# Decode steps kept on GpSimd, and the second groups' B and C projected before the last x tiles

## The chip, the cores and the metric

One core of a Trainium2 chip runs the whole program; the metric is device microseconds of one execution, and less is better. The core has a matrix engine (TensorE, PE in the rows; its weight loads are PEld), VectorE (DVE), ScalarE (ACT), GpSimd (POOL) and SyncE (SP), whose queue issues most DMAs. Each engine works through its own list of instructions in order and waits on semaphores for the others.

## The reference

One step of a hybrid layer (d_model 1024) for a prompt of 1024 positions and 8 decode requests of one position each, all with the same weights. Cut to what the change touches:

```python
proj = rmsnorm(x) @ w_in                       # columns: z (1536) | x,B,C (2048) | dt (24) | v (512)
xbc  = silu(causal_dwconv(xbc, width 4))       # x: 24 heads x 64; B, C: 4 groups x 64
y    = ssd_scan(x, dt, a, B, C, h0) + d_skip * x          # chunks of 128 positions
y    = rmsnorm(y * silu(z), per group of 384) * w
x    = x + concat(y, pooling(v)) @ w_out ;  then the convolutional FFN
```

For a decode request the scan is one step: `h = exp(dt*a)*h0 + dt*x*B`, `y = sum over the 64 states of h*C`, plus `d_skip*x`; `h` is an output. There are 12 tiles of x with 128 channels each, so 12 such steps on tiles of 128 x 8 requests x 64 states.

## The kernel before

Channels lie on the 128 partitions and the 1032 positions (1024 of the prompt, 8 of decode) in the free dimension. Every product is made of three float32r matmuls (high x high, high x low, low x high), L159 to L161. A projected tile is 128 output channels: three groups of 24 matmuls of 344 columns, 72 in all, and each group gets a PSUM bank (`g`) that ScalarE empties. The input tiles are numbered as in `w_in`: 0 to 11 are x, 12 and 13 are B, 14 and 15 are C, 16 to 27 are z (the gate tiles). Tile 12 and 14 serve the first half of the heads (x tiles 0 to 5), 13 and 15 the second half (x tiles 6 to 11).

`conv_tile` projects one of the tiles 0 to 15: weights are loaded (L130, SP), split into high and low parts (L140 on ScalarE, L141 on VectorE), projected, evacuated to `u` (L468 to L471, ScalarE), convolved into `xs` (L481 on ScalarE, then three L483 on VectorE), and passed through SiLU (L188, ScalarE). `gate_tile` projects a z tile, evacuates it (L656), applies SiLU and multiplies it into `xs` on VectorE (L661 for the prompt, L663 for the 8 decode columns). After every third gate tile a group norm adds up squares on GpSimd (L676) and sums them over partitions with matmuls (L683).

The scan over 8 chunks of 128 positions is done for the first half of the heads (q = 0) and then for the second (q = 1). For a chunk, `decay` loads a table of cumulated decays (`mix`, by DMA), clamps it on VectorE (L505), takes exponentials on ScalarE and multiplies the part for the incoming state (`ce`) by C on GpSimd (L520). `turn` transposes x, B and C on TensorE (L532, L538, L541). `apply` makes the chunk's products (L564, L587, L597), scales the state `h` on GpSimd (L573), adds to it on VectorE (L577), and adds the products to `xs` on VectorE (L605). A chunk's `ce` must be there before its L597, and `h` of the chunk before it too.

`sample_tile` is the decode step of one x tile: five operations on GpSimd (L636 to L639, L641, 128 x 512 elements except L636), a load and a store of the state `st`, and then on VectorE the sum over the 64 states (L642) and the skip term (L643). `st`, the scratch tile `stt` and the broadcast B and C (`bc`) have one buffer each. The tile `bcs`, through which B and C of a half reach DRAM (`sample_bc`, L617 on VectorE), uses the same buffer as `stt`.

`ssd_phase` sets the program's order. Scan steps and decode steps stand in a queue; before each of a tile's three groups of matmuls, `between` adds a credit and calls as many steps as whole credits allow. In the code's order: x tiles 1 to 5; the first half's chunks between the groups of x tiles 6 to 11; decode steps 0 to 5 between those of tiles 13 and 15; the second half's chunks, with decode steps 6 to 11 in steps 1 to 6 of them, between those of gate tiles 16 to 21. Gate tiles 22 to 27 and the pooling tiles follow outside the phase. A scheduler then fixes each engine's list from that order and its own estimate of times, so an engine's list is not the code's order; the lists are compared below.

```python
        for n in range(6, 12):
            self.keep(n, self.conv_tile(n, n, between))
        flush()
```

Of the kernel before, what the change touches and what calls it, by code (L numbers as in the profile page):

```python
# [13 lines left out]
ALU = mybir.AluOpType  # L14
AX = mybir.AxisListType
# [10 lines left out]
NST = 64  # L26
# [49 lines left out]
class Kernel:  # L76
# [543 lines left out]
    def sample_tile(self, q, i):  # L620

        nc, d = self.nc, self.d
        g = (i // 3) % 2
        if i % 3 == 0:
            self.bc = self.ph.tile([P, 2, NB, NST], F32, tag="bc", name=self.nm("bc"), bufs=1)
            for j in range(2):
                src = self.bcd[q : q + 1, :, j * P + g * NST : j * P + (g + 1) * NST]
                nc.sync.dma_start(self.bc[:, j], src.rearrange("o b n -> (o b) n").partition_broadcast(P))
        bb, cc = self.bc[:, 0], self.bc[:, 1]
        xt = self.xs_samp(self.xs[i])  # L630
        st = self.ph.tile([P, NB, NST], F32, tag="st", name=self.nm("st"), bufs=1)
        nc.sync.dma_start(st, d["st_ssm"][i])
        dx = self.ph.tile([P, 2, NB], F32, tag="dx", name=self.nm("dx"), bufs=2)
        tmp = self.ph.tile([P, NB, NST], F32, tag="stt", name=self.nm("stt"), bufs=1)
        bcast = lambda a: a.unsqueeze(2).broadcast_to([P, NB, NST])
        nc.gpsimd.tensor_tensor(out=dx[:, 0], in0=self.dtS[:, i, :], in1=xt, op=ALU.mult)  # L636
        nc.gpsimd.tensor_tensor(out=tmp, in0=bb, in1=bcast(dx[:, 0]), op=ALU.mult)
        nc.gpsimd.tensor_tensor(out=st, in0=st, in1=bcast(self.dA[:, i, :]), op=ALU.mult)
        nc.gpsimd.tensor_tensor(out=st, in0=st, in1=tmp, op=ALU.add)  # L639
        nc.sync.dma_start(d["ssm_s"][i], st)  # L640
        nc.gpsimd.tensor_tensor(out=tmp, in0=st, in1=cc, op=ALU.mult)  # L641
        nc.vector.tensor_reduce(out=dx[:, 1], in_=tmp, axis=AX.X, op=ALU.add)  # L642
        nc.vector.scalar_tensor_tensor(  # L643
            out=xt, in0=xt, scalar=self.c("dsk", i), in1=dx[:, 1], op0=ALU.mult, op1=ALU.add
        )

    def gate_tile(self, n, i, between):
        nc = self.nc
# [47 lines left out]
    def project(self):  # L696

        nc, d, tc = self.nc, self.d, self.tc
        self.bcd = self.dram.tile([2, NB, 2 * P], F32, name="bcd")
        self.xs, self.bt, self.ctl = [None] * XT, {}, {}  # L700

        with ExitStack() as outer:
            with self.banks(g=3, pT=2, pY=2, pM=1) as self.ps:
                self.startup([(n, n) for n in (12, 14, 0)])
                self.pu = outer.enter_context(tc.tile_pool(name="u", bufs=1))
                with tc.tile_pool(name="ssd", bufs=1) as self.ph:
                    self.ssd_phase()
            with self.banks(g=4, pT=2, pY=1, pM=1) as self.ps, tc.tile_pool(name="mix", bufs=1) as self.ph:
                for i in range(6, 12):
                    self.gate_tile(16 + i, i, None)  # L710
                self.pool_groups()

    def ssd_phase(self):
        nc, d = self.nc, self.d
        self.hst = {}
        queue = []

        credit = [0.0, 0.0]

        def between():  # L720
            credit[0] += credit[1]
            while credit[0] >= 1.0 and queue:
                credit[0] -= 1.0
                queue.pop(0)()
            if not queue:
                credit[0] = 0.0

        def flush():
            while queue:
                queue.pop(0)()  # L730

        def ssd_tasks(q):
            dec, trn = {}, {}

            def start():
                dec[0] = self.decay(q, 0)

            def step(c):
                if c >= 0:
                    self.apply(q, c, *dec.pop(c), *trn.pop(c))  # L740
                if c + 1 < NCH:
                    trn[c + 1] = self.turn(q, c + 1, dec[c + 1][0])
                if c + 2 < NCH:
                    dec[c + 2] = self.decay(q, c + 2)
                if c == -1:
                    self.sample_bc(q)
                if q == 1 and 1 <= c < 7:
                    sample(5 + c)

            queue.append(start)  # L750
            for c in range(-1, NCH):
                queue.append(lambda c=c: step(c))

        def sample(i):
            with self.behind(self.pl):
                self.sample_tile(i // 6, i)

        self.lo_eng = nc.gpsimd
        for n in range(1, 6):
            self.keep(n, self.conv_tile(n, n, None))  # L760
        ssd_tasks(0)
        credit[:] = 0.35, 0.6
        for n in range(6, 12):
            self.keep(n, self.conv_tile(n, n, between))
        flush()
        self.lo_eng = nc.vector
        for i in range(6):
            queue.append(lambda i=i: sample(i))
        credit[1] = 1.0
        for n in (13, 15):  # L770
            self.keep(n, self.conv_tile(n, n, between))
        flush()
        nc.sync.dma_start(d["conv_o"], self.conv_st)
        ssd_tasks(1)
        credit[:] = 0.35, 0.6
        for i in range(6):
            self.gate_tile(16 + i, i, between)
        flush()
        self.run_due()
# [789 lines left out]
```

## Time and profile before

| | us |
|---|---|
| median of 3 runs | 1425.16 (1421.04 to 1427.28) |
| the profiled execution | 1422.84 |
| its span, first to last instruction | 1421.1 |
| TensorE busy | 1364.8 (96%) |
| VectorE busy | 968.7 (68%) |
| ScalarE busy | 701.1 (49%) |
| GpSimd busy | 504.5 (36%) |

Times in the rows count from the start of the span. A matmul's record lasts longer than its share of the array, since matmuls are pipelined, so the pace is read from starts. The granted clock is a share of TensorE's full clock: 1.00 is 2.4 GHz and 0.50 is 1.2 GHz. The stretch that the change touches runs from about 232 us, after the last chunk of the first half, to about 407 us, after the last chunk of the second half.

### The profile page before, as it was taken

The numbers are of one execution on the slowest core, as the hardware profiler recorded it, in microseconds if no ns is written. First come the engines' busy times: TensorE is split into PE (matmuls) and PEld (weight loads), VectorE is DVE, ScalarE is ACT, GpSimd is POOL, SyncE is SP. The second block draws the span as 40 slices with busy tenths as digits, with TensorE's granted clock in tenths as the row PEclk, the third lists the DMA queues.
The fourth block names the chain that finished last, engine by engine and source line by source line (L and its number), as shares of the span: only waits on it lengthen the run. The fifth ranks groups of instructions, "written<-read, shape, count | busy, mean of one in ns | idle before, by whom it ended". The sixth has DMA issues, their size and how long they took to land.

```text
span 1421.1 us, 26585 instructions
## 1 busy us (share of the span) xinstructions
PE 1364.8 (96%) x10312; PEld 1313.3 (92%) x10312; DVE 968.7 (68%) x1474; ACT 701.1 (49%) x1408; POOL 504.5 (36%) x577
## 2 busy tenths in 40 slices
PE   8999999797999999999989999999999999999997
PEld 6899878786789999999978999999999999999997
DVE  6474899578853385563589777777777786567743
ACT  6247774276454543221455555545554555445451
POOL 5243466547631103776232222222122224214122
PEclk9999999999899999999999999999999999999999
DMA  6031334334311127776576878787777869657513
GB/s 246 9 100 56 102 113 164 120 116 127 127 40 40 34 76 265 237 236 220 152 196 146 219 194 203 192 195 180 182 196 201 202 202 324 223 185 236 179 54 120
DMA packets 126811, 227.56 MB, mean 160 GB/s; under 512 B 27980, under 2 KB 45212, under 8 KB 126684
## 3 DMA queue, kind: packets, MB, share of 16 engines
q1 hardware_dynamic: 86316, 139.39, 31.4%
q0 software_dynamic: 24336, 61.30, 17.6%
q10 hardware_dynamic: 16032, 25.16, 5.3%
q8 instruction: 81, 1.33, 0.4%
q14 instruction: 46, 0.38, 0.1%
HBM read 169.11 MB, written 45.15 MB: 151 GB/s over the span
## 4 chain that ended last, share of the span: by engine, by line
PE 79%; DVE 10%; DMA 4%; issue 3%; POOL 2%; ACT 1%; SPq 0%; DVEq 0%; ACTq 0%; POOLq 0%
PE g L1074 30%; PE g L1256 15%; PE g L160 10%; PE g L161 10%; PE g L159 10%; DMA mix<-acd 1%; DVE wop L141 1%; DVE xs L483 1%; DVE mix L550 1%; PE pY L587 1%; DMA st<-st_ssm 1%; DVE x L296 1%; DVE xs L605 1%; DVE mix L505 1%; POOL st L639 1%
## 5 line engine op out<-in xcount | busy, mean ns | idle before, releaser
L1074 PE MATMUL g<-op,wop 128*128 128x258 f32 x3696 | 445.3, 283 | 4.7 <-ACT op L999 1.7
L1074 PEld LDWEIGHTS g<-op,wop 128*128 128x128 f32 x3696 | 444.1, 189 | 5.7 <-DVE op L1004 2.0
L140 ACT ACTIVATE wop<-raw 128x512 fp32r<-128x512 f32 (+1 forms) x208 | 125.9, 608 | 225.3 <-PE g L161 131.9
L159 PE MATMUL g<-hh,wop 128*128 128x344 f32 x696 | 226.5, 325 | 4.4 <-ACT u L468 3.0
L1256 PE MATMUL g<-op,wop 128*128 128x258 f32 x1848 | 225.2, 283 | 2.4 <-ACT op L210 1.7
L1256 PEld LDWEIGHTS g<-op,wop 128*128 128x128 f32 x1848 | 222.7, 189 | 3.5 <-ACT op L210 1.9
L161 PE MATMUL g<-hh,wop 128*128 128x344 f32 x696 | 225.8, 324 | 0.0
L160 PE MATMUL g<-hl,wop 128*128 128x344 f32 x696 | 225.2, 324 | 0.0
L141 DVE TENSOR_TENSOR wop<-raw,wop 128x512 fp32r<-128x512 f32 (+1 forms) x186 | 141.3, 765 | 110.5 <-ACT wop L140 108.3
L140 ACT ACTIVATE wop<-s 128x512 fp32r<-128x512 f32 (+1 forms) x136 | 83.6, 620 | 139.6 <-PE g L1256 52.0
L159 PEld LDWEIGHTS g<-hh,wop 128*128 128x128 f32 x696 | 132.1, 190 | 7.6 <-ACT u L468 3.6
L161 PEld LDWEIGHTS g<-hh,wop 128*128 128x128 f32 x696 | 132.1, 190 | 1.9 <-issue 1.7
L160 PEld LDWEIGHTS g<-hl,wop 128*128 128x128 f32 x696 | 132.4, 190 | 0.7 <-issue 0.7
L1054 POOL DMA_DIRECT2D s<-s x44 | 38.3, 870 | 258.2 <-DVE wop L141 111.0
L1156 DVE SCALAR_TENSOR_TENSOR acc<-u,cst,acc 128x1048 f32<-128x1048 f32 x88 | 115.2, 1309 | 12.2 <-ACT acc L1154 10.6
L141 DVE TENSOR_TENSOR wop<-s,wop 128x512 fp32r<-128x512 f32 (+1 forms) x136 | 92.0, 682 | 36.2 <-ACT wop L140 34.2
L1134 DVE TENSOR_TENSOR u<-u,g 128x258 f32<-128x258 f32 (+2 forms) x176 | 58.0, 354 | 72.9 <-PE g L1074 66.1
L1131 ACT ACTIVATE u<-g 128x258 f32<-128x258 f32 (+2 forms) x220 | 69.6, 340 | 70.7 <-PE g L1074 70.6
L160 PE MATMUL g<-yl,wop 128*128 128x344 f32 x288 | 91.9, 320 | 1.6 <-DVE yl L211 1.6
L161 PE MATMUL g<-yh,wop 128*128 128x344 f32 x288 | 91.8, 320 | 0.0
L159 PE MATMUL g<-yh,wop 128*128 128x344 f32 x288 | 91.1, 320 | 0.0
L1226 POOL DMA_DIRECT2D g<-td x77 | 41.8, 548 | 122.3 <-DVE op L211 70.6
(269 smaller groups left out, 2278.2 us busy)
## 6 DMA issues: line engine op xcount, KB each, us to landing
s<-wup SPq DMA_DIRECT2D x88, 256.0 KB, 3.5
g<-td POOLq DMA_DIRECT2D x77, 258.0 KB, 4.7
raw<-wup SPq DMA_DIRECT2D x66, 256.0 KB, 4.1
raw<-win SPq DMA_DIRECT2D x58, 256.0 KB, 2.6
mix<-acd SPq DMA_DIRECT2D x16, 768.0 KB, 6.5
td<-acc ACTq DMA_DIRECT2D x22, 516.0 KB, 6.1
s<-wup POOLq DMA_DIRECT2D x44, 256.0 KB, 5.6
s<-s POOLq DMA_DIRECT2D x44, 256.0 KB, 3.9
```

The lines of the kernel that those rows point to most:

```text
L140: self.nc.scalar.activation(hi, raw[:, :w], AF.Copy)
L141: lo_eng.tensor_tensor(out=lo, in0=raw[:, :w], in1=hi.bitcast(F32), op=ALU.subtract)
L159: nc.tensor.matmul(ps[:, :n], wh, xh[:, sl], start=(first and k == 0), stop=False)
L160: nc.tensor.matmul(ps[:, :n], wh, xl[:, sl], start=False, stop=False)
L161: nc.tensor.matmul(ps[:, :n], wl, xh[:, sl], start=False, stop=(final and k == last))
L1054: nc.gpsimd.dma_start(t, raw[acc] if acc in raw else w[acc][j], accum_op=ALU.add)
L1074: nc.tensor.matmul(out, a, b, start=(p in OPENS and j == 1), stop=(j == 12), skip_group_check=True)
L1131: a = nc.scalar.activation(out, ps[:, s], AF.Copy, scale=-1.0 if p in ("p5", "p4") else 1.0)
L1134: nc.vector.tensor_tensor(out=out, in0=out, in1=ps[:, s], op=op)
L1156: nc.vector.scalar_tensor_tensor(out=acc, in0=u[:, k : k + FW], scalar=self.c("fw", 3 * n + k), in1=acc, op0=ALU.mult, op1=ALU.add)
L1226: self.loaded = self.nc.gpsimd.dma_start(st[:, j], self.td[i + j][ROW[p]]).ins
L1256: self.pe = nc.tensor.matmul(out, a, b, start=(s == 0 and i == 0 and j == 0), stop=(s == len(PIECES) - 1 and i == nk - 1 and j == 2),).ins
```

## The change

Three things. The decode step's last two operations leave VectorE: GpSimd sums the 64 states by six halving additions (32, 16, 8, 4, 2 and 1 wide) and makes the skip term with two more, eight instructions in place of two. Tiles 13 and 15 are projected among the first half's chunks, in place of x tiles 10 and 11, which come behind them with the decode steps, at a credit of 0.7 in place of 1.0 and with no flush. One gate tile (16) stands between x tile 11 and the second half's chunks, which lie between gate tiles 17 to 22; 23 to 27 remain outside.

```diff
-        nc.vector.tensor_reduce(out=dx[:, 1], in_=tmp, axis=AX.X, op=ALU.add)
-        nc.vector.scalar_tensor_tensor(
-            out=xt, in0=xt, scalar=self.c("dsk", i), in1=dx[:, 1], op0=ALU.mult, op1=ALU.add
-        )
+        w = NST
+        while w > 1:
+            w //= 2
+            out = dx[:, 1].unsqueeze(2) if w == 1 else tmp[:, :, :w]
+            nc.gpsimd.tensor_tensor(out=out, in0=tmp[:, :, :w], in1=tmp[:, :, w : 2 * w], op=ALU.add)
+        nc.gpsimd.tensor_scalar(out=xt, in0=xt, scalar1=self.c("dsk", i), scalar2=None, op0=ALU.mult)
+        nc.gpsimd.tensor_tensor(out=xt, in0=xt, in1=dx[:, 1], op=ALU.add)
...
-                for i in range(6, 12):
+                for i in range(7, 12):
                     self.gate_tile(16 + i, i, None)
...
-        for n in range(6, 12):
+        for n in (13, 15, 6, 7, 8, 9):
             self.keep(n, self.conv_tile(n, n, between))
         flush()
...
-        credit[1] = 1.0
-        for n in (13, 15):
+        credit[1] = 0.7
+        for n in (10, 11):
             self.keep(n, self.conv_tile(n, n, between))
-        flush()
         nc.sync.dma_start(d["conv_o"], self.conv_st)
+
         ssd_tasks(1)
+        self.gate_tile(16, 0, between)
         credit[:] = 0.35, 0.6
-        for i in range(6):
+        for i in range(1, 7):
             self.gate_tile(16 + i, i, between)
```

The new lines shift the code behind them by three or four: L661 and L663 become L664 and L666, L676 becomes L679, L683 becomes L686, L656 becomes L659.

On VectorE, this is a piece of the difference at the end of the first half's chunks, where the weights' low parts (`wop`), the convolution of the next tile (`xs_2421`) and the sums of decode steps 1 and 2 (`dx`, from `stt`) stand:

```order
-L505 SCALAR_TENSOR_TENSOR mix_2807<-acl,mix_2807 128x1536
-L642 TENSOR_REDUCE dx_2484<-stt_2485 128x8
-L643 SCALAR_TENSOR_TENSOR xs_784<-xs_784,cst,dx_2484 128x8
+L505 SCALAR_TENSOR_TENSOR mix_2935<-acl,mix_2935 128x1536
 L141 TENSOR_TENSOR wop_2567<-raw_2565,wop_2567 128x512
 L141 TENSOR_TENSOR wop_2572<-raw_2570,wop_2572 128x512
-L483 SCALAR_TENSOR_TENSOR xs_2421<-u_2298,cst,xs_2421 128x1056
-L642 TENSOR_REDUCE dx_2522<-stt_2523 128x8
-L483 SCALAR_TENSOR_TENSOR xs_2421<-u_2298,cst,xs_2421 128x1056
-L643 SCALAR_TENSOR_TENSOR xs_883<-xs_883,cst,dx_2522 128x8
-L483 SCALAR_TENSOR_TENSOR xs_2421<-u_2298,cst,xs_2421 128x1056
+L483 SCALAR_TENSOR_TENSOR xs_2421<-u_2298,cst,xs_2421 128x1056 x3
```

The sums are gone, and the three convolution steps follow each other.

On ScalarE, before, from the last convolved tile (`xs_2697`, tile 15, the second half's C) to the exponentials of the second half's chunks 0 and 1 (`mix_2742`, `mix_2807`); `z` is gate tile 16, `bT` is B transposed for chunk 0:

```order
L481 ACTIVATE xs_2697<-u_2575,cst 128x1056
L656 ACTIVATE z_2740<-g_2715 128x344
L188 ACTIVATE xs_2697<-xs_2697 128x1056
L181 ACT_TABLE_LOAD
L188 ACTIVATE mix_2742<-mix_2742,acl 128x128 x12
L656 ACTIVATE z_2740<-g_2758 128x344
L533 ACTIVATE bT_2786<-pM_2787 128x128
```

And after the change, where `xs_2697` is x tile 11, `z_2740` again gate tile 16, `z_2868` gate tile 17, and `mix_2870` and `mix_2935` belong to chunks 0 and 1:

```order
L481 ACTIVATE xs_2697<-u_2575,cst 128x1056
L659 ACTIVATE z_2740<-g_2715 128x344
L188 ACTIVATE xs_2697<-xs_2697 128x1056
L659 ACTIVATE z_2740<-g_2760 128x344
L140 ACTIVATE wop_2989<-raw_2987 128x512
L659 ACTIVATE z_2740<-g_2804 128x344
L140 ACTIVATE wop_2994<-raw_2992 128x512
L188 ACTIVATE z_2740<-z_2740 128x1032
L181 ACT_TABLE_LOAD
L188 ACTIVATE mix_2870<-mix_2870,acl 128x128 x12
L188 ACTIVATE mix_2935<-mix_2935,acl 128x128 x2
L659 ACTIVATE z_2868<-g_2843 128x344
```

A whole gate tile now lies between the last SiLU that the chunks need and the transposed B of chunk 0 (`bT`, some rows further on).

On TensorE the same place counts in matmuls: from the end of the first half's last chunk, 240 matmuls stood before the first transpose of the second half (L532) and 26 more before the first that needs C (L538); now 312 stand before L532 and L538 follows at once. From the second half's chunk 0 (L564) to its chunk 7, 307 matmuls of projections stood between the chunks, and 288 now.

On GpSimd, before, from the scaled state (`h`) of the second half's chunk 3 over decode step 8 (`dx_3409`, `st_3407`, `stt_3410`) to the state of chunk 4:

```order
L573 TENSOR_TENSOR h_3330<-h_3164,cd 128x384
L636 TENSOR_TENSOR dx_3409<-dtS,xs_1776 128x8
L638 TENSOR_TENSOR st_3407<-st_3407,dA 128x512
L520 TENSOR_TENSOR ce_3099<-ce_3099,xs_2697 128x768
L637 TENSOR_TENSOR stt_3410<-bc_3117,dx_3409 128x512
L676 TENSOR_TENSOR sq_3318<-sq_3318,sq_3319 128x1056
L639 TENSOR_TENSOR st_3407<-st_3407,stt_3410 128x512
L641 TENSOR_TENSOR stt_3410<-st_3407,bc_3117 128x512
L573 TENSOR_TENSOR h_3493<-h_3330,cd 128x384
```

And after the change, from decode step 7's product with C to the state of chunk 3:

```order
L641 TENSOR_TENSOR stt_3384<-st_3381,bc_3252 128x512
L646 TENSOR_TENSOR stt_3384<-stt_3384 128x8x32
L646 TENSOR_TENSOR stt_3384<-stt_3384 128x8x16
L646 TENSOR_TENSOR stt_3384<-stt_3384 128x8x8
L646 TENSOR_TENSOR stt_3384<-stt_3384 128x8x4
L646 TENSOR_TENSOR stt_3384<-stt_3384 128x8x2
L646 TENSOR_TENSOR dx_3383<-stt_3384 128x8
L648 TENSOR_TENSOR xs_2039<-xs_2039,dx_3383 128x8
L520 TENSOR_TENSOR ce_3234<-ce_3234,xs_1513 128x768
L679 TENSOR_TENSOR sq_3163<-sq_3163,sq_3164 128x1056
L573 TENSOR_TENSOR h_3486<-h_3305,cd 128x384
```

Seven more small operations (with L647, the skip term's product, further up) now stand ahead of the next chunk's `ce`, the group norm's sum and the next `h`.

## Rows read from the trace of the kernel before

**Rows 1.** The page's first line.

```profile
span 1421.1 us, 26585 instructions
```

**Rows 2.** Stretches: us; busy us of PE, PEld, DVE, ACT, POOL; granted clock; DMA.

```profile
232.50:274.00 41.50, 38.49 (x248) 37.84 (x241) 28.00 (x34) 13.35 (x24) 26.95 (x27) 1.00 0.46 141
274.00:283.90 9.90, 4.47 (x29) 4.16 (x27) 4.72 (x6) 1.10 (x2) 3.75 (x4) 0.96 0.44 140
283.10:289.90 6.80, 5.98 (x24) 5.76 (x25) 4.13 (x7) 6.77 (x19) 0.00 (x0) 0.50 0.01 2
293.40:407.00 113.60, 102.20 (x780) 84.02 (x780) 97.08 (x144) 63.99 (x134) 74.82 (x47) 0.89 0.38 119
320.70:327.50 6.80, 5.46 (x42) 3.66 (x43) 5.46 (x8) 5.32 (x15) 5.17 (x4) 0.50 0.13 47
378.80:395.80 17.00, 17.00 (x92) 11.74 (x90) 15.40 (x25) 9.62 (x19) 12.16 (x7) 0.50 0.37 127
407.00:720.00 313.00, 311.17 (x2035) 307.32 (x2033) 161.85 (x234) 117.29 (x191) 116.30 (x119) 1.00 0.47 151
```

**Rows 3.** Waits from 232 to 290 us: total us, times, longest us.

```profile
ACT xs L188 <- DVE xs L483: 38.3, 4, 10.1
DVE dx L642 <- POOL stt L641: 13.6, 4, 4.4
...
PE pT L538 <- ACT xs L188: 5.4, 1, 5.4
...
PE g L159 <- ACT u L468: 3.0, 2, 2.3
```

**Rows 4.** The chain that ended last, 278 to 287 us: start, us, what.

```profile
278.21 1.24 POOL stt L641
279.47 0.69 DVE dx L642
...
281.53 1.23 DVE xs L483
282.78 1.09 ACT xs L188
283.92 0.80 PE pT L538 x4
...
286.19 0.29 PE g L161
```

**Rows 5.** TensorE in order of time, first and last of 34 matmuls.

```profile
239.78 0.32 PE L159 MATMUL g<-hh,wop 128*128 128x344 f32 x1
...
244.98 0.32 PE L159 MATMUL g<-hh,wop 128*128 128x344 f32 x1
```

**Rows 6.** GpSimd by line, 290 to 410 us: busy us, mean ns, idle before.

```profile
L641 POOL TENSOR_TENSOR stt<-st,bc 128x512 f32<-128x512 f32 x6 | 11.8, 1970 | 0.4
...
L636 POOL TENSOR_TENSOR dx<-dtS,xs 128x8 f32<-128x8 f32 x6 | 2.5, 408 | 0.0
```

**Rows 7.** GpSimd, 225 to 285 us: one long product; ns min/median/max of the small one.

```profile
278.18 1.26 POOL L641 TENSOR_TENSOR stt<-st,bc 128x512 f32<-128x512 f32 x1
...
L636 POOL TENSOR_TENSOR dx<-dtS,xs x4: 209/398/1209, 239.3 to 264.1; 128x8 f32<-128x8 f32 x4
```

**Rows 8.** VectorE by line, 290 to 410 us.

```profile
L642 DVE TENSOR_REDUCE dx<-stt 128x8 f32<-128x512 f32 x6 | 4.1, 678 | 3.7 <-POOL stt L641 3.7
...
L643 DVE SCALAR_TENSOR_TENSOR xs<-xs,cst,dx 128x8 f32<-128x8 f32 x6 | 1.7, 278 | 0.0
```

**Rows 9.** VectorE in order of time: one operation twice, GpSimd idle, then busy.

```profile
347.42 1.76 DVE L505 SCALAR_TENSOR_TENSOR mix<-acl,mix 128x1536 f32<-128x1536 f32 x1 [3.02 <-DMA mix<-acd]
...
390.91 2.83 DVE L505 SCALAR_TENSOR_TENSOR mix<-acl,mix 128x1536 f32<-128x1536 f32 x1
```

**Rows 10.** Waits of TensorE from 225 to 425 us.

```profile
PE pY L597 <- POOL ce L520: 3.4, 1, 3.4
...
PE pM L532 <- DVE h L577: 2.8, 1, 2.8
```

## The prediction

> **What bounds the kernel now.** The first line of the page gives the span, 1421.1 us [rows 1]; the execution takes 1422.84 us, so 1.7 us lie around it. Next I cut the span into stretches [rows 2]. From 407 to 720 us TensorE is busy for 311.17 of 313.00 us at a granted clock of 1.00: there the matmuls themselves are the time, and whatever arrives there earlier is won in full. The pace is 0.158 us a matmul: 34 of them start between 239.78 and 244.98, 33 steps in 5.20 us [rows 5]. Before 407 us TensorE waits, in two places.
>
> The first is the end of the decode steps. From 274.00 to 283.90 us TensorE is busy for only 4.47 of 9.90 us [rows 2]. The waits of this stretch tell who is waited for [rows 3]: TensorE stands 5.4 us before the transpose that needs C (L538), waiting for ScalarE's SiLU of that tile, and 3.0 us for a bank that ScalarE has yet to empty (L468). ScalarE in turn stands 38.3 us, in four waits, for VectorE's convolution, and VectorE 13.6 us for GpSimd, at the sum over the states. The chain that ended last shows it link by link [rows 4]: GpSimd's product with C at 278.21, VectorE's sum at 279.47, the convolution to 282.76, SiLU at 282.78, TensorE's transpose at 283.92. VectorE takes its list in order, so the convolution of a tile waits for a decode step that has nothing to do with it. Then TensorE's clock is granted at 0.50, its lower level of 1.2 GHz, from 283.1 to 289.9 us [rows 2], right after the engine stood idle; a matmul takes 0.29 us there [rows 4].
>
> The second is the stretch of the second half's chunks, 293.4 to 407 us. No single engine fills its 113.6 us: VectorE is busy for 97.08 and GpSimd for 74.82 [rows 2], and they hand work to each other in every chunk. TensorE's list waits for `ce` from GpSimd (3.4 us) and for `h` from VectorE (2.8 us), among others [rows 10], and the clock is at 0.50 for 6.8 and 17.0 us [rows 2].
>
> **The change part by part.** *The sums and skip terms leave VectorE, and the order of tiles changes.* Both act on the first place, so I cost them together. With the sums gone, VectorE's convolution no longer waits for GpSimd; and tiles 13 and 15, whose B and C the transposes need, are done long before, while after the last x tile there are 48 + 72 matmuls, 120 x 0.158 = 19.0 us, before the first transpose. Undisturbed, SiLU follows a tile's last matmul after an evacuation, a step on ScalarE and three L483 of 1.23 us [rows 4]; I estimate 8 us, so it is covered. What goes is the 5.4 and the 3.0 us [rows 3], and half of the 5.98 busy us at 0.50 [rows 2], 3.0 us: **11.4 us**. The lower bound is nothing, if a new wait takes their place; the cover is 46 more matmuls (312 against 266), 7.3 us, and if the decode steps ended so late that this were used up, GpSimd's list would hold the chunks' `ce` back. Before, GpSimd's last product of the six steps ended at 279.4 [rows 7], and its waits for VectorE go while the additions come, so I expect it to end near 285 us, with the first transpose at 232.5 + 312 x 0.158 = 281.8 and the first `ce` needed some ten us later.
>
> *Eight small operations on GpSimd in place of two on VectorE.* The trace has no such addition. From below: a small operation on 128 x 8 takes 0.209 us undisturbed, and a 128 x 512 product 1.26 us [rows 7], so 1.05 us for 504 elements; the six additions write 256 + 128 + 64 + 32 + 16 + 8 = 504. Eight starts and those elements are 8 x 0.209 + 1.05 = 2.7 us. From above: among the chunks these rows' means are 1.970 and 0.408 us [rows 6], and 8 x 0.408 + 1.56 = 4.8 us. Should each small operation take the 1.209 us of the slowest one [rows 7], it is 8 x 1.209 = 9.7 us. Six steps lie in the second half's chunks: 16 to 29 us on GpSimd, 58 at the far end. GpSimd has 113.6 - 74.8 = 38.8 us idle there [rows 2], so the additions fit on the whole, but `ce`, the group norm's sum and `h` stand behind them in its list, and I take the rate among chunks, 4.8 us, as the nearer end.
>
> VectorE loses 6 x (0.678 + 0.278) = 5.7 us and its 3.7 us of waits for GpSimd [rows 8]. Against that, L505 takes 1.76 us beside an idle GpSimd and 2.83 us beside a busy one [rows 9]: 1.07 us more for an overlap with about one long product. One more such overlap a step is 6 x 1.07 = 6.4 us, which takes back the 5.7. The Trainium skill, "GPSIMD Engine Reference", Key points, says that GpSimd shares its SBUF interfaces with VectorE and contends with VectorE instructions of two SBUF inputs; this trace agrees, with 2.83 against 1.76 us. With 6.4 against 5.7, only the waits are gone on VectorE, 3.7 us, and I let GpSimd's later `ce` and `h` eat half: **1.9 us**. The 19 matmuls fewer between the chunks (288 against 307) run later instead, at no change.
>
> *DMA queues.* The same loads and stores are issued. In SyncE's list some tables of decays now stand behind the store of a decode step's state, which waits for GpSimd; the store comes ahead of the six additions, so this hangs on GpSimd's pace again, and I put it at nothing beyond that.
>
> *Gate tile 16 ahead, 22 inside.* TensorE does the same matmuls; moved they cost nothing where TensorE is full.
>
> Sum: 11.4 + 1.9 = 13.3 us, and 1422.84 - 13.3 = 1409.5 us. The profiled execution lies 2.3 us under the median of the runs, 1425.16, so as a median I predict **1412 us**.
>
> **The rivals.** All times are medians, 1425.16 and the named terms.
>
> *GpSimd takes back the most of it.* The additions make `ce` and `h` late in the last chunks, and the stretch becomes 8 us longer in place of 1.9 shorter: 1425.2 - 11.4 + 8 = 1421.8. For it: GpSimd would be busy for 74.8 + 29 = 104 of 113.6 us [rows 2, 6], and TensorE already waits 3.4 us for a `ce` [rows 10]. Against it: at 2.7 us a step it is 91.
>
> *The wait only moves.* VectorE meets GpSimd again at L666, the decode columns' gate, and at L617, whose tile shares a buffer with the scratch tile; the 8.4 us of idle [rows 3] stay and the rest goes: 1425.2 - 3.0 - 1.9 = 1420.3. Against it: each gate comes some tiles after its decode step, and L617 needs GpSimd's sixth step at about 285 us and stands behind the first chunk's products.
>
> *GpSimd becomes the bound: slower.* At 9.7 us a step GpSimd needs 74.8 + 58 = 133 us for the stretch of 113.6, 19 more, and 1425.2 - 11.4 + 19 = 1433. It decides where the additions use up half of the 38.8 idle us and then the 11.4 won before, 31 us in six steps, from about 5 us a step. For it: the small operation's 1.209 us [rows 7]. Against it: the mean of six among the chunks is 0.408 [rows 6]. The skill's "GPSIMD Engine Reference", Engine selection, speaks for it: a sum along the free dimension belongs on VectorE, and two-input elementwise work is about twice as slow on GpSimd. This trace has VectorE's sum at 0.678 us, and no row for GpSimd's.
>
> *More is won.* If the chunks flow better and the clock stays up, half of the 6.8 and 17.0 us at 0.50 [rows 2] is won as well, up to 12 us: 1400.
>
> **How the numbers follow.** The forecast has 0.56, more won 0.11, taken back 0.18, moved 0.06, slower 0.09. A measurement of this kernel tells a change from none from about 0.5%, 7.1 us: 1418 and 1432. Faster: 0.56 + 0.11 = 0.67; within: 0.18 + 0.06 = 0.24; slower: 0.09. The forecast's own range is 1405 to 1418 (additions at 2.7 us, or the stretch 4 us longer). The range for 8 in 10 reaches from 1400, the case of more won, to 1425, beyond the cases within the bound; what is left out is the slower case and half of the low end.
>
> **What would show it.** Right: VectorE has no wait for GpSimd and ScalarE's waits for the convolution shrink from 38.3 us to under 15; TensorE goes from the first half's last chunk to the first transpose at about 282 us without the wait of 5.4, and the clock holds at 1.00 to 300 us; L646 takes 0.2 to 0.7 us, eight operations 2.7 to 4.8 in a step; the last chunk's products end near 404 us with 49 more matmuls behind them. Wrong: GpSimd busy for over 105 us of the chunks' stretch, with waits of TensorE for `ce` or for the group norm's sum (L686) of over 10 us; a second stretch at 0.50 as long as before would show that its cause is not what left VectorE.

## The result, and the profile after

The changed kernel takes 1416.55 us, the median of seven runs (1412.1 to 1424.72), against 1425.15 us for the kernel before. The ratio of the runs is 0.9947, with a 95% interval of 0.9924 to 0.997. That is faster by 7.6 us, with 4.3 and 10.8 us as the interval's ends. The prediction was 1412 us and 13.3 us faster.

The profiled execution took 1417.17 us. The first lines of its page answer to [rows 1] and to the table of the section before:

```profile
span 1415.4 us, 26675 instructions
...
PE 1357.8 (96%) x10312; PEld 1307.4 (92%) x10312; DVE 968.1 (68%) x1450; ACT 701.6 (50%) x1408; POOL 565.2 (40%) x673
```

GpSimd works 60.7 us more than before. VectorE has lost its twelve sums and twelve skip terms and is busy for as long as before (968.1 against 968.7 us).

The stretches, which answer to [rows 2]. The columns are each engine's busy time with its number of instructions, then the granted clock, the DMA share and GB/s:

```profile
231.40:280.90 49.50, 49.50 (x324) 49.33 (x317) 34.60 (x31) 23.10 (x45) 47.36 (x58) 1.00 0.36 114
280.90:296.20 15.30, 11.44 (x92) 10.32 (x90) 6.28 (x10) 10.63 (x22) 14.12 (x23) 0.99 0.36 124
295.90:299.30 3.40, 3.08 (x11) 1.90 (x12) 3.40 (x6) 0.49 (x1) 3.40 (x3) 0.50 1.04 368
296.20:406.70 110.50, 93.55 (x730) 76.97 (x734) 92.07 (x129) 58.09 (x126) 100.78 (x95) 0.89 0.41 126
```

The first row is the whole way from the first half's last chunk to the first transpose of the second half: TensorE is busy for all of its 49.50 us. The waits of 5.4 and 3.0 us of [rows 3] are gone. But GpSimd is busy for 47.36 us of the same row and goes on so in the next, where TensorE works for 11.44 of 15.30 us. The last row is the stretch of the second half's chunks: GpSimd is busy for 100.78 of 110.50 us.

The waits from 232 to 300 us, which answer to [rows 3] (line, what it waited for, total, times, longest):

```profile
ACT xs L188 <- DVE xs L483: 22.2, 4, 8.8
...
DVE bcs L617 <- POOL dx L646: 6.3, 1, 6.3
...
PE pM L564 <- DVE bcs L617: 3.9, 1, 3.9
```

The place where the second half begins, in order of time (start, duration, engine, line, what, and in brackets the idle time before it and what ended that):

```profile
291.76 0.34 SPq L640 DMA_DIRECT2D ssm_s<-st  x1
291.82 1.26 POOL L641 TENSOR_TENSOR stt<-st,bc 128x512 f32<-128x512 f32 x1
...
293.16 2.28 POOL L646 TENSOR_TENSOR stt<-stt 128x256 f32<-128x256 f32 x5
...
295.52 0.20 POOL L646 TENSOR_TENSOR dx<-stt 128x8 f32<-128x8 f32 x1
295.75 0.41 DVE L617 COPY bcs<-pM 8x256 f32<-8x256 f32 x1 [6.26 <-POOL dx L646]
...
296.22 1.55 PE L564 MATMUL pM<-xd,bT 128*64 128x384 f32 x4 [3.88 <-DVE bcs L617]
```

GpSimd sums the sixth decode step until 295.7 us. `bcs` uses the buffer of that step's scratch tile, so VectorE stands for 6.26 us at L617. TensorE stands for 3.88 us before chunk 0's products for the state (L564): they are written into `pM`, of which there is one bank, and it still holds the transposed B and C that L617 has to copy out. Then the clock is granted at 0.50, 1.2 GHz, for 3.4 us (the row 295.90:299.30).

In the chunks behind it these are TensorE's longest waits, which answer to [rows 10]:

```profile
PE g L159 <- ACT z L659: 6.4, 2, 5.6
...
PE pY L587 <- DVE mix L550: 3.7, 2, 2.2
PE pT L686 <- POOL sq L679: 2.6, 2, 1.6
PE pY L587 <- ACT z L188: 2.4, 1, 2.4
PE pY L597 <- POOL ce L520: 1.8, 1, 1.8
```

### The profile page after: what moved, and what is told of

Read it like the earlier page. It is cut to its first block, busy times and chain, and to the rows that moved or that the text cites. A ratio compares the mean times of both kernels' runs of the same rounds, so it can differ in the third digit from the quotient of the medians.

```text
span 1415.4 us, 26675 instructions
## 1 busy us (share of the span) xinstructions
PE 1357.8 (96%) x10312; PEld 1307.4 (92%) x10312; DVE 968.1 (68%) x1450; ACT 701.6 (50%) x1408; POOL 565.2 (40%) x673
## 5 line engine op out<-in xcount | busy, mean ns | idle before, releaser
L1135 ACT ACTIVATE u<-g 128x258 f32<-128x258 f32 (+2 forms) x220 | 69.6, 340 | 68.9 <-PE g L1078 68.8
```

Of the source, the lines that this page charges most:

```text
L1135: a = nc.scalar.activation(out, ps[:, s], AF.Copy, scale=-1.0 if p in ("p5", "p4") else 1.0)
```

## The experiments

Each run is compared with runs of the kernel before on the same chip; 0.001 of a ratio is 1.4 us. Repeats of one kernel spread over 6 to 13 us, so that the intervals of the ratios are 1.6 to 3.5 us wide on either side. For the place of a loss I use the traces. The table gives, for one profiled execution of each kernel, the time of a stretch less 0.158 us for each of the projections' matmuls that start in it (counted in the trace): what the stretch costs beyond the projections. "To chunk 0" runs from the last product of the first half's chunks (L597) to the first L564 of the second half; "chunks" from there to the last L597; "behind" from there to the first matmul of the FFN. From that matmul on, where all kernels do the same, the executions take 687.0 to 693.0 us; that is the spread to bear in mind. Ahead of the first column they differ as well: it starts between 230 and 235 us, latest with the order of tiles alone. The columns come from one execution of each kernel, and no run shows how far they repeat.

| kernel | to chunk 0 | chunks | behind | sum | ratio to before (95%) |
|---|---|---|---|---|---|
| before | 16.9 | 62.5 | 5.0 | 84.4 | |
| the change | 8.0 | 65.0 | 6.2 | 79.2 | 0.9947 (0.9924 to 0.9970) |
| sums on GpSimd alone | 16.5 | 63.2 | 7.9 | 87.6 | 0.9996 (0.9983 to 1.0009) |
| order of tiles alone | 11.3 | 59.8 | 5.9 | 77.0 | 0.9959 (0.9943 to 0.9974) |
| late sums on VectorE | 7.6 | 61.2 | 5.9 | 74.7 | 0.9928 (0.9903 to 0.9952) |
| early sums on VectorE | 12.7 | 63.7 | 9.2 | 85.6 | 0.9964 (0.9951 to 0.9977) |
| sums 2 to 5 on GpSimd | 5.7 | 64.1 | 5.5 | 75.3 | 0.9949 (0.9931 to 0.9967) |
| `bcs` in the buffer of `cb` | 4.0 | 65.3 | 9.1 | 78.4 | 0.9943 (0.9924 to 0.9963) |
| `bcs` in a buffer of `ce` | 4.0 | 68.8 | 5.1 | 77.9 | 0.9960 (0.9941 to 0.9979) |
| late sums on VectorE, `bcs` in `ce` | 4.0 | 69.7 | 8.1 | 81.8 | 0.9954 (0.9936 to 0.9972) |
| no gate tile ahead | 5.6 | 79.4 | 11.0 | 96.0 | 1.0057 (1.0039 to 1.0074) |
| late additions doubled | 7.9 | 72.4 | 5.6 | 85.9 | 0.9994 (0.9982 to 1.0005) |
| decode steps 6 to 11 left out | 7.9 | 51.3 | 6.8 | 66.0 | 0.9858 (0.9838 to 0.9879) |

### The sums on GpSimd alone

The kernel before, with the first part of the change and nothing else:

```diff
-        nc.vector.tensor_reduce(out=dx[:, 1], in_=tmp, axis=AX.X, op=ALU.add)
-        nc.vector.scalar_tensor_tensor(... dsk ...)
+        (the six halving additions and the two operations of the skip term, on nc.gpsimd)
```

> The kernel before with one part alone: the sums and skip terms on GpSimd, the tiles in their old order. My theory: both parts act on the waits at the end of the first six decode steps, so this part alone wins a part of it. ScalarE's waits for the convolution fall from 38.3 us to under 15, and the 5.4 us before the transpose that needs C and the 3.0 us for a bank mostly go; the additions among the second half's chunks (about 4.6 us a step on GpSimd) give back some 4 us. 1425 - 8.4 + 4 = about 1421 us. Rival, the order is all that counts: the sums on GpSimd are a cost alone, TensorE waits at the same transpose for a SiLU that is as late, and the time is 1425 to 1430 us.

1423.9 us, ratio 0.9996: nothing is won. My 1421 us was too good and the reason in it incomplete, and ScalarE's waits for the convolution fell to 29.1 us and not under 15. TensorE's waits from 225 to 420 us:

```profile
PE pM L564 <- DVE bcs L617: 10.4, 1, 10.4
PE pT L686 <- POOL sq L679: 3.9, 1, 3.9
PE pM L532 <- DVE h L577: 3.3, 2, 3.1
...
PE pT L538 <- ACT xs L188: 0.5, 1, 0.5
```

The wait at the transpose that needs C fell from 5.4 to 0.5 us, as expected. It came back at L617, where VectorE stood for 11.76 us for GpSimd's sixth step. That is the rival "the wait only moves", at the place that it named and at more than its price (10.4 us against 8.4). Nor is the picture of this run's own rival right, that the sums change nothing at the transpose.

### The order of tiles alone

The changed kernel with VectorE's two operations back in `sample_tile`.

> The changed kernel with the sums and skip terms back on VectorE, so the new order of tiles alone. My theory: tiles 13 and 15 are done before the decode steps begin, so the transposes wait for nothing, and VectorE's waits for GpSimd only delay x tile 11, which a gate tile of 72 matmuls covers (11.4 us); the second half's chunks are spared the additions. 1425 - 10 = about 1414 us, level with the full change or 2 to 3 us better. Rival, the sums on VectorE are what counts: the convolutions of x tiles 10 and 11 stand behind the sums, ScalarE empties banks late, and TensorE waits 5 us or more somewhere from 240 to 290 us: 1420 us or more.

1418.76 us, ratio 0.9959: it wins most of the whole. That is 4 to 5 us short of the 1414 us that I expected. The rival's waits for banks are there, 5.4 us in TensorE's waits from 235 to 303 us, but not its time of 1420 us or more:

```profile
PE g L159 <- ACT u L468: 3.0, 2, 2.2
PE g L159 <- ACT z L656: 2.4, 1, 2.4
```

and in ScalarE's of the same stretch:

```profile
ACT xs L188 <- DVE xs L483: 38.2, 4, 10.1
```

ScalarE waits as long for the convolutions as before (38.3 us, [rows 3]), and TensorE for banks. So the two parts of the change take away different waits: the order takes that before C's transpose, the sums on GpSimd take those for banks, and bring the one at L617. That the sums add anything to what the order wins is not shown: the intervals of the two ratios overlap (0.9943 to 0.9974 and 0.9924 to 0.9970), and in the table's executions the order alone costs less than the whole change (77.0 against 79.2 us).

### The tile `bcs` in another buffer

```diff
-        s = self.ph.tile([NB, 2 * P], F32, tag="stt", name=self.nm("bcs"), bufs=1)
+        s = self.ph.tile([NB, 2 * P], F32, tag="cb", name=self.nm("bcs"), bufs=1)
```

> The changed kernel, with the tile for B and C (L617) in the buffer of cb in place of the decode step's scratch tile. My theory: VectorE's 6.3 us wait for GpSimd's sixth decode step goes, the 4.2 us in which TensorE stands before chunk 0's products (L564) go with it, and so does the half clock behind it: 4 to 6 us faster than the changed kernel, 1411 to 1412.5 us. Rival, the wait only moves: GpSimd is as late, chunk 1's ce or the low part of a weight is late in its place, and the time stays within 1.5 us of the changed kernel's 1416.5.

The ratio is 0.9943, level with the change (0.9947) and not 4 to 6 us faster: the wait only moves, as the rival said. The same kernel once more, for its profile:

> The run with the tile for B and C in a buffer of its own once more, for its profile. My theory now: GpSimd ends the first six decode steps at 296 us all the same, and chunk 1's ce stands behind them; so the wait of 4.2 us before chunk 0 (L564) is gone, and TensorE stands about as long for chunk 1, at L587 or L597 for ce or h. Rival: no such wait shows from 290 to 310 us, and the lost time is elsewhere, in the later chunks.

It took 1413.94 us, one run. The wait before chunk 0 is gone (the first column of the table falls from 8.0 to 4.0), and chunk 1 waits instead, but for another reason than I gave. VectorE's waits from 290 to 310 us:

```profile
DVE cb L543 <- DMA bcd<-bcs: 3.8, 1, 3.8
```

I had only put `bcs` into the way of the next mask `cb`, which stands until `bcs` is stored. So a buffer of `ce` was tried, which is needed again only in chunk 2:

```diff
+        s = self.ph.tile([NB, 2 * P], F32, tag="ce", name=self.nm("bcs"), bufs=2)
```

> The changed kernel with the tile for B and C (L617) in one of the two buffers of ce, where neither GpSimd nor a later tile is waited for soon (in the buffer of cb, chunk 1's mask stood 3.8 us behind the store of B and C). My theory: the wait of 4 us before chunk 0 goes and no other takes its place within two chunks; TensorE is some 4 us further at chunk 1 than in the changed kernel, and the time is about 1413 us. Rival, GpSimd's end at 296 us moves the wait to chunk 1's ce: within 1.5 us of the changed kernel, with a wait for ce (L520) of 3 us or more from 295 to 312 us.

The ratio is 0.996. Up to chunk 1 it goes as I expected: from 280 to 303 us TensorE is busy without a pause, at full clock.

```profile
280.00:303.00 23.00, 23.00 (x172) 20.54 (x170) 14.09 (x24) 14.22 (x30) 21.82 (x30) 1.00 0.50 167
```

But the next column of the table gives back what the first won (68.8 against 65.0 us). On VectorE, and then in the waits of SyncE's queue from 280 to 310 us:

```profile
297.24 0.96 DVE L545 TENSOR_TENSOR xd<-xd,wd 128x768 f32<-128x768 f32 x1
303.98 2.60 DVE L505 SCALAR_TENSOR_TENSOR mix<-acl,mix 128x1536 f32<-128x1536 f32 x1 [5.77 <-DMA mix<-acd]
```

```profile
SPq L640 <- POOL st L639: 13.8, 2, 7.4
```

VectorE stands 5.77 us for the table of decays (`mix`) of chunk 2. Its load stands in SyncE's list behind the store of the sixth decode step's state (L640), for which SyncE waits 7.4 us, until GpSimd has computed that state; the store goes out at 292.13 and the table's load only at 296.99 us. Neither my theory nor its rival named this. GpSimd's decode steps hold the chunks by two ways at the same time: VectorE's L617 through a buffer, and the decay tables through SyncE's queue. Taking one away leaves the other. No run takes away the second way alone, so its price is not measured.

### The late sums back on VectorE

```diff
+        if q:
+            (VectorE's two operations)
+        else:
             (GpSimd's eight)
```

> The changed kernel with the sums and skip terms back on VectorE for decode steps 6 to 11 alone, which lie among the second half's chunks; steps 0 to 5 keep them on GpSimd. My theory: GpSimd loses about 6 x 4.6 = 28 us of work in that stretch, the group norm's sum (L679) and ce come earlier, TensorE's waits of about 6 us for a bank and 2.6 us for the group norm shrink by half, and VectorE takes on 6 x 0.96 us and some waits: about 3 us faster than the changed kernel, 1413 to 1414 us. Rival, the additions among the chunks cost nothing, since GpSimd has room there: within 1.5 us of 1416.5, or slower by VectorE's waits for GpSimd, 1418 us.

The ratio is 0.9928, the lowest of all kernels that compute the reference: 3 us under the change, as expected, but the intervals overlap (0.9903 to 0.9952 and 0.9924 to 0.9970), so that it is not shown to be faster. The trace agrees, with 61.2 us in the chunks against 65.0, and the busy times of that stretch:

```profile
298.70:405.50 106.80, 92.74 (x734) 76.85 (x734) 99.18 (x141) 59.34 (x128) 73.34 (x48) 0.92 0.42 132
```

GpSimd has 27 us less to do, VectorE 7 us more, and TensorE's waits for a `z` bank and for the group norm's sum are 1.0 us together with none at L686 left; those for `h` (L532) and for `mix` (L587) are longer than after the change, 6.2 and 5.9 us against 0.2 and 3.7. SyncE's waits for GpSimd's state, from 225 to 410 us, are 53.5 us before, 80.3 after the change and 64.1 here. The line of each, in this order:

```profile
SPq L640 <- POOL st L639: 53.5, 8, 10.7
```

```profile
SPq L640 <- POOL st L639: 80.3, 10, 11.6
```

```profile
SPq L640 <- POOL st L639: 64.1, 10, 8.8
```

### The opposite, and a part of the early sums

The same switch the other way round (GpSimd's eight for steps 6 to 11 alone), and one that puts the sums of steps 0 and 1 on VectorE as well as the late ones (`if i < 2 or q`).

> The changed kernel with the sums and skip terms on VectorE for decode steps 0 to 5, on GpSimd for steps 6 to 11, the opposite of the run with the late sums on VectorE. My theory: as with the order alone, some 5.6 us are won before chunk 0 (TensorE still waits 6 us for banks, because convolutions stand behind sums), no wait at L617, and the additions among the chunks cost what they cost there, 2 to 3 us and the group norm's wait behind: 1425 - 5.8 + 3 to 5 = 1421 to 1424 us. Rival, the additions among the chunks cost nothing: as the order alone, 1418 to 1420 us.

> The changed kernel with the sums and skip terms on VectorE for decode steps 0 and 1 and 6 to 11, on GpSimd for steps 2 to 5 alone. My theory: in the changed kernel GpSimd works without a pause from 231 to 296 us on the first six steps, and its end there (10.8 us a step) is what the second half's chunk 0 and 1 wait for (L617, then ce). Two of six sums less end its list near 287 us, before anybody needs it, and VectorE's two early sums stand ahead of no late convolution: the 3.5 to 4.2 us before chunk 0 are gone, on top of what the late sums on VectorE won: 1417.2 - 3.5, less some 0.5 us, 1412 to 1415 us, the best of all. Rival, the chunks' stretch eats it (TensorE waits at the next transposes for h or for the decays instead): 1416 to 1418 us.

With the early sums on VectorE the ratio is 0.9964, 1419.5 us: in the rival's range and not in mine, level with the order alone (0.9959), so that these two kernels show no price of the late additions. Its trace has the bank waits back before chunk 0 (12.7 us in the first column, 11.3 with the order alone) and one wait of 10.1 us for the group norm's sum (L685 of that kernel) on GpSimd in the column behind. With sums 2 to 5 alone on GpSimd the wait at L617 shrinks from 3.9 to 1.6 us and the first column is at 5.7, but the time is that of the change, 0.9949: what was won before chunk 0 does not show in the ratio. By the ratio the rival was right, with its waits for `h` (L532, 5.8 us) and at L587 (6.7 us); the time itself, 1415.59 us, lies between the two figures.

### Both remedies together

> The kernel with the sums of steps 6 to 11 back on VectorE, and with the tile for B and C in a buffer of ce as well. My theory: both remedies add up, since one acts before chunk 0 (4 us) and the other behind it (about 3 us): 1411 us, a ratio to the kernel before of about 0.990. Rival: the wait goes to chunk 1, and it is level with the late sums alone, 0.993.

0.9954. They don't add up. Chunk 0 comes 4 us earlier and the chunks behind it take 69.7 us. The wait at chunk 2's table is there as well (VectorE stands 5.96 us for it at L505), and TensorE waits 4.8 us for a `z` bank although the late sums are on VectorE.

### Without the gate tile ahead

```diff
-        self.gate_tile(16, 0, between)
         credit[:] = 0.35, 0.6
-        for i in range(1, 7):
+        for i in range(6):
```

> The changed kernel without its third part: no gate tile between x tile 11 and the second half's chunks, which lie between gate tiles 16 to 21 again. My theory: the 72 matmuls (11.4 us) of that tile are the cover for the end of GpSimd's first six decode steps. Without it the first transposes come some 11 us earlier, at about 270 us, GpSimd ends as late as 294 to 296, and TensorE stands 10 us or more before chunk 0's products (L617, as with the sums alone): 1421 to 1425 us, all or most of the gain gone. Rival, tiles 13 and 15 ahead are what won the time, and the cover is not needed: 1416 to 1418 us.

1431.1 us, 1.0057: slower than before, and a bigger loss than the 1421 to 1425 us that I expected, but not where I expected it. The first transposes come at 284.8 us, behind 336 matmuls, since the first six decode steps still stand ahead of them in the queue; the wait at L617 is 0.6 us. The loss is at the other end. The queue holds 16 calls, and the 24 groups of matmuls have credit for 15 of them: 4 from 6 x 0.7, and 11 from 0.35 + 18 x 0.6. With the gate tile's three groups there is credit for all 16. Without them the last chunk is called with nothing left to do beside it. The stretch of its products:

```profile
404.50:415.10 10.60, 4.94 (x40) 3.44 (x36) 4.77 (x7) 1.08 (x1) 9.09 (x10) 0.50 0.12 41
```

TensorE works for 4.94 of 10.60 us, at a clock of 0.50, and GpSimd for 9.09: a `ce` stands there behind decode step 11, and TensorE waits 5.7 us for it. So the third part of the change is not a cover for the early decode steps alone: its groups of matmuls are also what the late chunks are spread over.

### The late additions doubled

The six halving additions of steps 6 to 11 are made a second time, on the scratch tile when the sum is stored.

> The changed kernel with the six halving additions made twice in decode steps 6 to 11 (the second set works on the scratch tile after the sum was stored, and changes no result). It adds some 6 x 3.4 = 20 us to GpSimd in the second half's chunks, where it is busy for about 100 of 110 us. My theory: GpSimd has no room left there, so ce, h and the group norm's sum come later by about the half of it, and the time is 8 to 15 us longer than the changed kernel's 1416.5: 1424 to 1432 us. Rival, GpSimd's spare time still takes it, since the waits for it are few: up to 3 us longer, under 1420 us.

1422.88 us, 0.9994: by the ratios 6.7 us over the change, where I had expected 8 at least and the rival 3 at most. In the chunks, 72.4 against 65.0 us:

```profile
296.10:414.10 118.00, 95.64 (x734) 78.34 (x734) 92.30 (x129) 58.13 (x126) 111.97 (x123) 0.84 0.38 119
```

GpSimd is at 95% there. The late additions come to 20.6 / 6 + 2.5 / 5 + 16.8 / 5 = 7.3 us a step (the last step's sum and its second set lie behind 414 us) and 8.2 with the skip term, and at that price all that the change wins is used up.

### Decode steps 6 to 11 left out

> The changed kernel with decode steps 6 to 11 left out altogether (the decode outputs of half of the heads are not computed), to price them among the second half's chunks. My theory: they load GpSimd with six steps of about 12 us and slow VectorE beside them, and the stretch from chunk 0 to chunk 7, which takes about 20 us more beyond its projections than the first half's (65 against 42), loses half of that: 1404 to 1408 us. Rival, that stretch is bound by the hand-over from chunk to chunk and the clock, and GpSimd's decode steps are hidden: within 4 us of the changed kernel, 1413 us or more.

1401.77 us, 0.9858. The chunks' stretch costs 51.3 us beyond its projections and not 65.0:

```profile
294.50:391.30 96.80, 89.02 (x730) 74.12 (x734) 79.74 (x129) 58.57 (x127) 29.76 (x17) 0.95 0.29 95
```

No instruction of VectorE is gone (129 as after the change), and it works 79.74 and not 92.07 us. So six decode steps on GpSimd, with their loads and stores, are worth about 13 us here, of which the additions are some part. It is a bound on what a better place for the late steps could bring; none was tried.

## Why the prediction was right, and where it was not

**The convolution no longer waits, and C is there in time: right.** The first transpose came at 280.92 us (281.8 foretold), 0.2 us ahead of the one that needs C, and TensorE never waited on the way. ScalarE's waits for the convolution fell to 22.2 us, not under 15; TensorE waited for none of them. The half clock at 283.1 us is gone.

**GpSimd's end at 285 us: this step failed.** The prediction let the six steps end near 285 us, without a sum, and they ended at 296 us. Even its lower rate of 2.7 us gives 279.4 + 6 x 2.7 = 295.6 us, less GpSimd's waits for VectorE that go, and these were 6.8 us in the trace before, from 225 to 300 us:

```profile
POOL stt L637 <- DVE dx L642: 6.8, 4, 3.1
```

That leaves 288.8 us, and the lower rate did not hold. GpSimd worked without a pause from 231.4 us on, 10.8 us a step. The early additions took (6.6 + 5.2 + 3.5 + 3.0 + 1.3 + 2.0) / 6 = 3.6 us and the skip term 1.09 + 0.37, about 5.1 us a step, more than among the chunks. The lower rate is met where VectorE stands idle at L617: the sixth step's additions and its last skip operation take 2.3 + 0.2 + 0.2 us at 293 to 296 us.

GpSimd's groups that carry this, from 231 to 297 us (line, shape and count, then total and mean ns):

```profile
L646 POOL TENSOR_TENSOR stt<-stt 128x256 f32<-128x256 f32 x6 | 6.6, 1092 | 0.4
...
L646 POOL TENSOR_TENSOR stt<-stt 128x128 f32<-128x128 f32 x6 | 5.2, 859 | 0.5
...
L647 POOL TENSOR_SCALAR xs<-xs,cst 128x8 f32<-128x8 f32 x4 | 4.4, 1088 | 0.1
L646 POOL TENSOR_TENSOR stt<-stt 128x64 f32<-128x64 f32 x6 | 3.5, 580 | 0.4
L646 POOL TENSOR_TENSOR stt<-stt 128x32 f32<-128x32 f32 x6 | 3.0, 503 | 0.5
...
L648 POOL TENSOR_TENSOR xs<-xs,dx 128x8 f32<-128x8 f32 x6 | 2.2, 375 | 0.4
L646 POOL TENSOR_TENSOR dx<-stt 128x8 f32<-128x8 f32 x6 | 2.0, 332 | 0.4
...
L646 POOL TENSOR_TENSOR stt<-stt 128x16 f32<-128x16 f32 x6 | 1.3, 218 | 0.5
```

So the first term, 11.4 us, is 16.9 - 8.0 = 8.9 us by the traces, and the rival "the wait only moves", which had 0.06, came true in part, at L617. It cost 3.9 us of waiting and 3.4 us at half clock. Against that rival the prediction had set L617 behind the first chunk's products; it stands ahead of L564 and empties the bank that L564 needs.

**4.8 us a step among the chunks: right.** (19.0 + 2.4) / 6 + 0.98 + 0.30 = 4.8 us in the trace.

**1.9 us won among the chunks: wrong in sign by the traces.** The stretch costs 65.0 and not 62.5 us beyond its projections, 2.5 us lost; with the late sums on VectorE it is 61.2. In the runs the price of the late additions is not clear of the noise: 0.9928 against 0.9947 with the early sums on GpSimd, 0.9959 against 0.9964 with them on VectorE. Only doubled do they show, with 6.7 us. VectorE's waits for sums are gone, and the 6.4 us by which its operations were to grow did not come. Its busy time in the chunks, 95.92 us before (below) and 92.07 after, fell by 3.9 us where 5.7 us of operations left:

```profile
295.40:406.40 111.00, 99.60 (x756) 81.97 (x752) 95.92 (x139) 62.02 (x131) 72.43 (x47) 0.89 0.39 120
```

What the trace shows in place of a gain is a new wait of 5.6 us, at 354 to 360 us, for a bank that ScalarE empties behind VectorE's L666. Followed back over VectorE's L695, ScalarE's exponentials and VectorE's L505 at 339.78 us, it comes from L550, L545 and L550 at 331 to 337 us, which take 1.67 + 3.19 + 1.58 us beside GpSimd's L520, L679 and L573. The additions are not its cause alone, since TensorE waits 4.8 us for such a bank in the run with both remedies too. TensorE's half clock from 280 us on is 23.9 us in all, against 30.7 before: the 6.8 us ahead of the chunks became 3.4 at their start, and the 23.9 among them became 20.5. Most of it did not go, it moved.

**DMA queues at nothing beyond GpSimd's pace: wrong by what was left unsaid.** SyncE waits 80.3 us for states against 53.5, and behind one such wait stands the table that chunk 2 needs; with L617 out of the way VectorE waits 5.8 us for it.

**The gate tile, moved at no cost: right as a term, but it is no small part.** Without it the kernel is slower than before by 8 us.

**The slower rival's point, about 5 us a step: too low.** The doubled additions, at 8.2 us a step in the late half, meet the old time. The rule that spoke for it (the Trainium skill, "GPSIMD Engine Reference", "4.1 Engine selection": sums along the free dimension on VectorE) agrees with the late half, 0.9928 with its sums on VectorE against 0.9947. It does not with the early one, 0.9959 with all sums on VectorE against 0.9928, where GpSimd's sums free VectorE's list. Both pairs of intervals overlap, so neither is shown beyond the noise.

Sum by the traces, to the FFN: 84.4 - 79.2 = 5.2 us, as the terms give it: 8.9 - 2.5 - 1.2. The profiled executions differ by 5.7 us, and the runs by 7.6, within the spread. The direction and the first term were right; that the time fell into the forecast's own range owes something to luck, since 1425.2 - 5.2 = 1420 us, the sum by the traces, lies outside of 1405 to 1418.

Of the prediction's signs of being right, the transposes came as foretold. The others failed: VectorE waits 6.3 us for GpSimd, ScalarE waits 22.2 us, the clock falls at 295.9 us, the eight operations take 5.1 us a step in the early half (4.8 among the chunks), and the last chunk's products end at 407 us and not near 404. Of its signs of being wrong, GpSimd stayed under 105 us among the chunks, at 100.78, and TensorE's waits for `ce` and at L686 were 4.4 us and not over 10; but a stretch of 6.8 us at 0.50 came again among the chunks, as long as before, so its cause is not what left VectorE.

What stays open is whether the sums on GpSimd add anything to the new order, whether 0.9928 is a real gain on 0.9947, and why 4 us won before chunk 0 don't show in the ratio of the kernels with `bcs` elsewhere: the waits at chunks 1 and 2 are shown in single executions, their price in the mean of many is not.

## What to carry to other kernels

When work moves to an engine that has idle time on the whole, follow its list from the place where it begins, at the dearest rate that the trace has for its small operations: what counts is when its last operation ends, and who then needs its buffers or stands behind its stores in a DMA queue. When a wait is taken away, look in the same trace for the second one that hangs on the same late engine, since taking one away alone may win nothing. And test the parts of a change one by one: here one part alone won nothing, one won three quarters and cannot be told from the whole by these runs, and leaving out the third turned the whole into a loss.

## What the runs showed of the hardware

A small GpSimd operation that starts beside a VectorE operation with two SBUF inputs lasts until that one ends, however few its elements. Of the changed kernel, GpSimd's and VectorE's rows at the same time:

```profile
240.70 1.73 POOL L636 TENSOR_TENSOR dx<-dtS,xs 128x8 f32<-128x8 f32 x1
```

```profile
240.26 2.10 DVE L505 SCALAR_TENSOR_TENSOR mix<-acl,mix 128x1536 f32<-128x1536 f32 x1 [0.95 <-DMA mix<-acd]
```

GpSimd's 8 columns end at 242.43 us, just behind VectorE's L505 at 242.36; the same operation takes 0.21 us at 280.09, where VectorE waits. From 225 to 410 us of the thirteen profiled executions, 35 GpSimd operations on 128x8 start during an L483 of VectorE, 0.15 us or more before its end; each ends 0.06 to 0.20 us behind it. Beside VectorE's copies out of PSUM the wait does not show: L648 takes 0.21 us at 329.82, beside an L542 from 329.62 to 330.18. It goes the other way too: beside GpSimd's sum of squares, VectorE's L545 takes 3.19 us, against 0.96 (297.24 us, above, in the run with `bcs` in a buffer of `ce`), and ends 0.8 us behind it:

```profile
331.78 3.15 POOL L679 TENSOR_TENSOR sq<-sq,sq 128x1056 f32<-128x1056 f32 x1
```

```profile
332.55 3.19 DVE L545 TENSOR_TENSOR xd<-xd,wd 128x768 f32<-128x768 f32 x1
```

The Trainium skill, "SBUF — State Buffer", section "SBUF: two separate sides", says that VectorE, in an operation with two SBUF inputs, and GpSimd take the shared pair of ports as an exclusive lock for the whole instruction. These rows agree, and the prediction had only priced it as a mean. By this, a sum split into six instructions can wait for the pair up to six times. Sum and skip term took 4.8 to 5.1 us a step beside VectorE, and seven of these eight operations 2.7 us where VectorE stood idle.
